# Operand buffers of layer 0's output projection: moved into layer 0's input space and kept open into layer 1

## The chip, the cores and the metric

The kernel runs on one core of one Trainium2 chip. The metric is the device time of one execution in microseconds; the comparison is between medians of several executions. The five engines are written as in the profile: PE (matmul), PEld (its weight load), DVE (vector), ACT (scalar), POOL (GpSimd), SP (sync, which here only issues loads).

## What is computed

Two layers of a diffusion trunk run over 128 context tokens and 1024 latent tokens, in float32. Around the change the work is this:

```python
# layer 0, output side; y_a from the SSD scan, y_b from the Hyena convolution
y_a = rms_norm(y_a * silu(z_a), norm_a_w)
xs  = xs + g_s * (concatenate([y_a, y_b], axis=-1) @ w_out)     # 2048 -> 1024
# layer 1, input side
h = rms_norm(xs, norm_w[1]) * (1.0 + sc) + sh
q, k, v, g = split(h @ w_in, 4, axis=-1)                        # 1024 -> 4 x 1024
# then 2-D neighbourhood attention with a bias table, o * silu(g), output projection,
# xs = xs + g_s * (...), final rms_norm
```

## The kernel before

**Numbers.** Every large product is made in three matmuls: an operand `x` is split into a high part (ACT's cast to `fp32r`) and a low part (DVE's subtraction `x - high`), and high·high, low·high and high·low are summed in PSUM. Weights stream in as 128x1024 blocks through two `wraw` buffers (`w_load`, L119); `w_split` (L125) makes their two halves (ACT L131, DVE L132). Activations are kept with channels on the partitions, as eight tiles of 128 x 1152 tokens.

**Buffers.** SBUF is handed out in pools, which are stacked from the left and from the right. A pool that is closed gives its bytes to the pools opened next; the first instructions that write into a new pool wait for all accesses to every pool whose bytes it takes, not only for those to the same bytes. Within a pool, a tag with `bufs=n` is a ring of n buffers, and a writer waits for the last use of the buffer that it gets.

**Order.** The program is emitted as one list. Before it goes to the chip, the queue of each engine is planned: in simulated time an engine takes, of what is ready, what was emitted first. On the chip each engine then works strictly through its queue. So a statement that is moved in the source changes who goes first where several things are ready. Loads are issued by SP, stores by POOL (`dma`, L85; `store`, L88).

**Start and layer 0.** `open` (L195) makes the pools that live throughout and loads the constants (`csq`, `pv`, `sel4`, `sel8`). Layer 0's input `h` is 16 tiles, `hh0`–`hh7` and `hl0`–`hl7`, in the pool `h` (53,120 to 126,848 bytes of each partition); products are evacuated through the pool `ev` above it (126,848 to 145,576). The last product of layer 0's input side is `x0g_main` (L894), which stores the eight tiles of the Hyena branch in `ybd`, apart from tile 6, which stays on the chip as `y6`. After its first group it calls `second` (L1587), and so `ssd_open` (L915), which loads the small mask `sm`, and starts the SSD scan (`ssd`, L976). The scan is a generator in the background list `bg`: `tick` (L92) advances it a few steps after each third of a product, so that DVE and ACT work on it while PE does the product.

**Output projection, stage out0a and out0b (L1602–1671).** `h` and `ev` are closed, and the pool `x1` takes the place: eight tiles of the residual stream, and the norm's small tiles and row scale `tt` with the diagonals `diag` (53,120 to 96,256). Behind it lie `yt` (two `yr` buffers, to 105,472) and `yb` (four `yhi` and four `ylo`, 105,472 to 142,336), so that `yb` reaches into the bytes of `ev`. `y_tile` (L1076) loads a tile of `y` into `yr` and splits it (L1086) into `yhi` and `ylo`. `out0` (L1096) runs over the four quarters of the 2048 input channels: quarter 3 and 2 from `ybd` (part 0 and 1), then the two of the scan (part 2 and 3), for which `mid` (L1612) drains the scan and builds its normalisation, and the pool `ya` on the right side holds eight split pairs. Each part runs over the eight output tiles `m`; `evac` adds the product times the gate to `x1[m]`. In part 2 the residual is loaded into `yr` and added (L1125).

**Layer 1's norm, in the last part.** `tail` squares each evacuated block of 384 columns into `sq1` (pool `yn`) and adds it up in `acc`. With the last output tile, per block: `token_sums` (L374) puts tokens on partitions, DVE makes the mean (`ms`), POOL the power -1/2 (`rs`), and `spread` (L362) brings it back to rows: DVE makes a diagonal (L366), PE multiplies it by ones (L369), ACT copies it out (L372). `tok(k)` (L1647, `to_tokens` at L698) turns an `x1` tile to tokens: nine PE transposes (L709), ACT's and DVE's copies (L712, L714) into `x1k` (pool `xk`), and a store to `x1d`, which the last stage of the kernel reads.

**Stage h1 (L1679).** Per tile `make_h` (L379) runs on DVE and ACT: two products with the row scale, into `sq` (L385, pool `hn`), ACT's high half, DVE's low half. The tiles `hh`, `hl` of layer 1 lie in the pool `h1` on the right. Behind the tiles 3 to 7 follows `tok(k)`.

**Stage qkv (L1208).** The pools of the output projection are closed, and `qk` and `at` are opened over them. `attn_open` (L1159) makes the two bias tables `Tb`: a memset of the whole table and one of its middle, for each half (L1165, L1166). For the first pair of heads `qkv` then makes the `q` and `k` weights, and splits the next two blocks, those of the value product, into the buffers of attention (`vw`, `QH`, `QL`), which aren't in use yet:

```python
if j == 0:
    first = [(evq, self.w_next(), [self.pj() for b in range(3)]),
             (evk, self.w_next(), [self.ps() for b in range(3)])]
    w = self.t(p_a, [128, 2, 1024], "vw", F32R, bufs=1)
    self.w_split(self.wpos, (w[:, 0], w[:, 1]))
    self.w_split(self.wpos + 1, [self.t(p_a, [128, 1024], n, F32R, bufs=1) for n in ("QH", "QL")])
    self.proj_k(first, self.hh, self.hl)
```

`proj_k` (L169) multiplies tile by tile as `make_h` delivers them (L186–188). Then `v_proj` (L1180) makes the values (L1191–1193) and attention runs in the background (`attn`, L1282; its context scores are L1330). `load_tables` (L1169) writes the windows of the bias into `Tb`.

Of the kernel before, what the change touches and what calls it, by code (L numbers as in the profile page):

```python
# [7 lines left out]
F32 = mybir.dt.float32  # L8
F32R = mybir.dt.float32r
AF = mybir.ActivationFunctionType  # L10
# [37 lines left out]
class Net:  # L48
# [146 lines left out]
    def open(self):  # L195
# [19 lines left out]
        self.dma(self.sel4, i["sel4"])  # L215
        self.sel8 = self.t(self.p_c, [128, 8], "sel8")
# [698 lines left out]
    def ssd_open(self, pool):  # L915
        nc = self.nc
        V = nc.vector
        sm = self.t(pool, [128, 12], "sm", bufs=1)
        self.dma(sm, self.i["sm"])
        self.sm = sm  # L920
        self.L = self.t(pool, [128, 8, 128], "L", F32R, bufs=1)
        self.Mv = self.t(pool, [128, 4, 128], "Mv", F32R, bufs=1)
        V.tensor_copy(self.L[0:64], bc(sm[0:64, 4:12].unsqueeze(2), [64, 8, 128]))
# [152 lines left out]
    def y_tile(self, src, k, p_y, pool, norm=None, r=None):  # L1076
        nc = self.nc
        if r is None:
            r = self.t(pool, [128, T], "yr")
            self.dma(r, src)  # L1080
        if norm is not None:
            nw = self.pv[:, PV["naw"] + k:PV["naw"] + k + 1]
            nc.vector.scalar_tensor_tensor(out=r, in0=r, scalar=nw, in1=norm, op0=ALU.mult, op1=ALU.mult)
        return self.split(r, p_y)

    def split(self, r, p_y, tags=("yhi", "ylo")):  # L1086
        nc = self.nc
        hi = self.t(p_y, [128, T], tags[0], F32R)
        lo = self.t(p_y, [128, T], tags[1], F32R)
# [118 lines left out]
    def qkv(self, p_a, p_q):  # L1208
# [3 lines left out]
        for j in range(8):  # L1212
# [11 lines left out]
            if j == 0:  # L1224
# [5 lines left out]
                self.w_split(self.wpos + 1, [self.t(p_a, [128, 1024], n, F32R, bufs=1) for n in ("QH", "QL")])  # L1230
                self.proj_k(first, self.hh, self.hl)
# [215 lines left out]
    def run(self, upto="end"):  # L1447
# [158 lines left out]
        x1 = [self.t(p_x1, [128, T], f"x1_{m}") for m in range(8)]  # L1606
        yst = ExitStack()
        pool = yst.enter_context(self.pool("yt", bufs=2))
# [3 lines left out]
        def mid():  # L1612
            self.drain()
            self.nd = 1
            rep = self.rstd_rep(self.ssq, p_x1, D)
# [12 lines left out]
        with self.pool("yb", bufs=4) as p_y:  # L1628
            self.label("out0a")
            ys = [self.y_tile(self.ybd[k], k, p_y, pool) for k in (4, 5, 7)]  # L1630
            ys.insert(2, self.y6)
            self.tick(self.EX)
            self.rate = self.RO
            self.out0(0, ys, x1, pool, order=(2, 0, 1, 3))
            ys = [self.y_tile(self.ybd[k], k, p_y, pool) for k in range(4)]
            self.out0(1, ys, x1, pool, mid=mid)
# [3 lines left out]
        acc = self.t(p_x1, [128, T], "tt", bufs=1)  # L1640
        psum = self.ps()
        ms = self.t(p_x1, [128, NCH], "ms", bufs=1)
        rs = self.t(p_x1, [128, NCH], "rs", bufs=1)
        self.nd = 1
        p_k = yst.enter_context(self.pool("xk", bufs=4))
        with self.pool("yn") as pn:
            def tok(k):  # L1647

                self.to_tokens(x1[k], self.x1d[:, :, k * 128:(k + 1) * 128].rearrange("c t n -> t c n"), p_k, "x1k", 4, both=True)()

            def tail(m, b, sl):
                if m == 0:
                    nc.scalar.activation(acc[:, sl], x1[m][:, sl], AF.Square)
                    return
                sq = self.t(pn, [128, NB], "sq1", bufs=3)
                nc.scalar.activation(sq, x1[m][:, sl], AF.Square)
                V.tensor_tensor(out=acc[:, sl], in0=acc[:, sl], in1=sq, op=ALU.add)
                if m == 7:

                    cs = slice(3 * b, 3 * b + 3)  # L1660
                    if b == 2:
                        tok(0)
                    self.token_sums(psum, acc, range(3 * b, 3 * b + 3))
                    V.tensor_scalar(out=ms[:, cs], in0=psum[:, cs], scalar1=1.0 / D, scalar2=EPS, op0=ALU.mult, op1=ALU.add)
                    nc.gpsimd.tensor_tensor(out=rs[:, cs], in0=ms[:, cs], in1=self.mh[:, cs], op=ALU.pow)
                    if b == 2:
                        tok(1)
                        tok(2)
                    self.spread(acc, rs, b, p_x1)

            self.out0(3, ya[4:], x1, pool, tail)
# [7 lines left out]
        with self.pool("hn") as pool:  # L1679
            self.label("h1")  # L1680
            self.hh, self.hl = [], []
            for k in range(8):
# [8 lines left out]
        with self.pool("at", bufs=2) as p_a:  # L1691
            self.attn_open(p_a)
# [218 lines left out]
```

## Time and profile before

| | us |
|---|---|
| runs | 2070.71, 2075.44, 2075.98 (median 2075.44) |
| profiled execution | 2070.57 |
| its span | 2068.8 |
| around the span | 1.77 |

| stretch (us from the start of the span) | work | PE busy |
|---|---|---|
| 840–1075 | `x0g`, the scan begins | 231.91 of 235.00 |
| 1075–1160 | out0a, the scan beside it | 82.28 of 85.00 |
| 1160–1327 | rest of the output projection | 161.19 of 167.00 |
| 1327–1358 | h1, first q and k products | 30.00 of 31.00 |
| 1358–1376 | the value product begins | 10.85 of 18.00 |
| 1376–1960 | values, attention, gates | 583.73 of 584.00 |

A row of a timeline gives the start, the mean duration, the engine, line and operation, output and inputs by the program's names, partitions times elements, how many such instructions are taken together, and in brackets how long the engine stood before it and what ended that. A row of the table by stretch gives, behind the length, the busy time and the count of instructions of PE, PEld, DVE, ACT and POOL, then the mean clock that was granted to PE (1.00 is full), the DMA engines' share and GB/s.

### The profile page before, as it was taken

The numbers are of one execution on the slowest core, as the hardware profiler recorded it, in microseconds if no ns is written. First come the engines' busy times: TensorE is split into PE (matmuls) and PEld (weight loads), VectorE is DVE, ScalarE is ACT, GpSimd is POOL, SyncE is SP. The second block draws the span as 40 slices with busy tenths as digits, with TensorE's granted clock in tenths as the row PEclk, the third lists the DMA queues.
The fourth block names the chain that finished last, engine by engine and source line by source line (L and its number), as shares of the span: only waits on it lengthen the run. The fifth ranks groups of instructions, "written<-read, shape, count | busy, mean of one in ns | idle before, by whom it ended". The sixth has DMA issues, their size and how long they took to land. (4 is left out here: it accounts for less than half of the span.)

```text
span 2068.8 us, 33792 instructions
## 1 busy us (share of the span) xinstructions
PE 2008.6 (97%) x13032; PEld 1815.4 (88%) x13032; DVE 1316.3 (64%) x2717; ACT 910.1 (44%) x2080; POOL 111.2 (5%) x235
## 2 busy tenths in 40 slices
PE   5999999999999999999999999989999999999998
PEld 3999997889999999888888899888888888888977
DVE  6887745146778787998899774743444444455374
ACT  4766642253333323554467411434544545454242
POOL 0010001110000000000000000100000000000000
PEclk9999999999999999999999999999999999999999
DMA  9142348554212113433343441233333233333362
GB/s 350 39 157 87 108 170 303 193 175 165 93 58 79 58 63 98 169 118 132 113 169 108 141 156 41 80 120 85 94 108 87 71 93 94 111 114 114 133 240 82
DMA packets 114344, 256.99 MB, mean 124 GB/s; under 512 B 27231, under 2 KB 62567, under 8 KB 111719
## 3 DMA queue, kind: packets, MB, share of 16 engines
q1 hardware_dynamic: 98872, 192.27, 28.9%
q0 software_dynamic: 15312, 62.57, 8.1%
q8 instruction: 103, 1.69, 0.3%
q14 instruction: 57, 0.47, 0.1%
HBM read 187.50 MB, written 67.28 MB: 123 GB/s over the span
## 5 line engine op out<-in xcount | busy, mean ns | idle before, releaser
L159 PE MATMUL pj<-hh,whi 128*128 128x384 f32 x1728 | 602.1, 348 | 3.4 <-DVE acc L880 2.9
L160 PE MATMUL pj<-hl,whi 128*128 128x384 f32 x1728 | 586.8, 340 | 0.0
L161 PE MATMUL pj<-hh,wlo 128*128 128x384 f32 x1728 | 586.4, 340 | 0.0
L159 PEld LDWEIGHTS pj<-hh,whi 128*128 128x128 f32 x1728 | 325.1, 188 | 25.0 <-issue 18.7
L160 PEld LDWEIGHTS pj<-hl,whi 128*128 128x128 f32 x1728 | 325.2, 188 | 7.5 <-issue 6.6
L161 PEld LDWEIGHTS pj<-hh,wlo 128*128 128x128 f32 x1728 | 324.7, 188 | 5.0 <-issue 4.2
L132 DVE TENSOR_TENSOR wlo<-wraw,whi 128x1024 fp32r<-128x1024 f32 x106 | 129.4, 1222 | 160.7 <-ACT whi L131 160.3
L131 ACT CAST whi<-wraw 128x1024 fp32r<-128x1024 f32 x106 | 111.1, 1049 | 247.8 <-PE pj L160 228.2
L1274 DVE CUSTOM_DVE_ANT_0 sz<-bg,Tb 128x512 f32<-128x512 f32 x128 | 83.5, 687 | 131.2 <-PE bg L1339 130.3
L613 ACT COPY raw<-pj 128x384 f32<-128x384 f32 (+2 forms) x140 | 55.9, 402 | 172.6 <-PE pj L161 83.8
L159 PE MATMUL pj<-yhi,whi 128*128 128x384 f32 x324 | 111.0, 343 | 1.4 <-DVE x L1110 1.4
L1276 ACT ACTIVATE sz<-sz,mx 128x512 f32<-128x512 f32 x128 | 91.6, 717 | 46.8 <-DVE mx L1274 46.4
L161 PE MATMUL pj<-yhi,wlo 128*128 128x384 f32 x324 | 110.4, 341 | 0.0
L160 PE MATMUL pj<-ylo,whi 128*128 128x384 f32 x324 | 109.2, 337 | 0.0
L1370 ACT COPY Pt<-bg 128x512 f32<-128x512 f32 (+1 forms) x144 | 71.8, 548 | 32.8 <-PE bg L1368 29.0
L1368 PE MATMUL bg<-csq,sz 128*128 128x128 f32 x528 | 73.9, 280 | 0.0
L942 ACT ACTIVATE xw<-xt,wd 128x64 f32<-128x64 f32 x256 | 64.5, 336 | 8.7 <-PE bg L949 8.0
L1368 PEld LDWEIGHTS bg<-csq,sz 128*128 128x128 f32 x528 | 56.7, 141 | 13.1 <-issue 13.0
L1110 DVE SCALAR_TENSOR_TENSOR x<-pj,mod,x 128x128 f32<-128x128 f32 (+1 forms) x96 | 46.6, 512 | 28.3 <-PE pj L161 24.3
L159 PEld LDWEIGHTS pj<-yhi,whi 128*128 128x128 f32 x324 | 60.9, 188 | 4.0 <-issue 3.3
L1191 PE MATMUL pj<-whi,hh 128*128 128x256 f32 x216 | 63.3, 293 | 0.0
L161 PEld LDWEIGHTS pj<-yhi,wlo 128*128 128x128 f32 x324 | 60.9, 188 | 1.3 <-issue 1.2
(445 smaller groups left out, 4073.2 us busy)
## 6 DMA issues: line engine op xcount, KB each, us to landing
wraw<-in_we SPq DMA_DIRECT2D x52, 512.0 KB, 3.4
wa<-in_wadg SPq DMA_DIRECT2D x32, 512.0 KB, 6.6
wraw<-in_wo SPq DMA_DIRECT2D x24, 512.0 KB, 3.5
Tb<-Cd SPq DMA_DIRECT2D x256, 48.0 KB, 2.0
Hd<-H POOLq DMA_DIRECT2D x8, 1280.0 KB, 5.2
H<-Hd SPq DMA_DIRECT2D x8, 1280.0 KB, 6.9
xt<-xtd SPq DMA_DIRECT2D x17, 512.0 KB, 4.2
wraw<-in_woe SPq DMA_DIRECT2D x16, 512.0 KB, 3.6
```

Of the source, the lines that this page charges most:

```text
L131: self.nc.scalar.copy(hi, r)
L132: self.nc.vector.tensor_tensor(out=lo, in0=r, in1=hi.bitcast(F32), op=ALU.subtract)
L159: nc.tensor.matmul(p[:, :NB], wh, xh[k][:, sl], start=(k == 0), stop=False)
L160: nc.tensor.matmul(p[:, :NB], wh, xl[k][:, sl], start=False, stop=False)
L161: nc.tensor.matmul(p[:, :NB], wl, xh[k][:, sl], start=False, stop=(k == nk - 1))
L613: nc.scalar.copy(raw[:, d], p[:, lo:hi])
L942: nc.scalar.activation(xw[:, h * 64:h * 64 + 64], x[:, h * 64:h * 64 + 64], AF.Copy, scale=self.wd[:, c, o:o + 1])
L1191: nc.tensor.matmul(p[:, :256], self.hh[k][:, ts], hi[:, q:q + 256], start=(k == 0), stop=False)
L1274: V.tensor_tensor_reduce(out=z[:, :n], in0=s, in1=tb, scale=-1.0, scalar=3.0e38, op0=ALU.add, op1=ALU.min, accum_out=m1)
L1276: nc.scalar.activation(z[:, :n], z[:, :n], AF.Exp, bias=m1, scale=-1.0, accum_out=sm)
L1368: nc.tensor.transpose(pt[:, b * 128:(b + 1) * 128], p[:, b * 128:(b + 1) * 128], self.ident)
L1370: nc.scalar.copy(t[:, :nb * 128], pt[:, :nb * 128])
```

## The change

Six edits go together.

1. `sm` is loaded in `open`, into the pool of constants, and no longer in `ssd_open`.
2. A pool `yb` is opened directly behind the eight `x1` tiles, so that it takes the second half of `h`'s bytes; the norm's small tiles go to a pool `xs` behind it. `yb` stays open until layer 1's input is made.
3. The first three `y` tiles (4, 5, 7) are loaded into `ylo` itself, and the low part is made in place. The others still go through `yr`.
4. The squares of `tail`, the row-scaled tiles of `make_h` and the token tiles take buffers of `yb` (`ylo`, `ylo`, `yhi`, four each) in place of pools of their own (`yn` with three, `hn` with two, `xk` with four).
5. A block's `spread` is emitted after the next block's sums; with the last block come blocks 1's spread, `tok(1)` to `tok(3)`, then block 2's spread. `tok(3)` no longer stands in h1.
6. `attn_open`, with its memsets, is emitted inside `qkv`, behind the two weight splits.

```diff
@@ open
+        self.sm = self.t(self.p_c, [128, 12], "sm")
+        self.dma(self.sm, i["sm"])
         self.sel8 = self.t(self.p_c, [128, 8], "sel8")
@@ ssd_open
-        sm = self.t(pool, [128, 12], "sm", bufs=1)
-        self.dma(sm, self.i["sm"])
-        self.sm = sm
+        sm = self.sm
@@ y_tile
+        if r is None and pool is None:
+            lo = self.t(p_y, [128, T], "ylo", F32R)
+            self.dma(lo.bitcast(F32), src)
+            return self.split(lo.bitcast(F32), p_y, lo=lo)
@@ split
-    def split(self, r, p_y, tags=("yhi", "ylo")):
+    def split(self, r, p_y, tags=("yhi", "ylo"), lo=None):
         hi = self.t(p_y, [128, T], tags[0], F32R)
-        lo = self.t(p_y, [128, T], tags[1], F32R)
+        if lo is None:
+            lo = self.t(p_y, [128, T], tags[1], F32R)
         nc.scalar.copy(hi, r)
         nc.vector.tensor_tensor(out=lo, in0=r, in1=hi.bitcast(F32), op=ALU.subtract)
@@ qkv
                 self.w_split(self.wpos + 1, [self.t(p_a, [128, 1024], n, F32R, bufs=1) for n in ("QH", "QL")])
+                self.attn_open(p_a)
                 self.proj_k(first, self.hh, self.hl)
@@ run, output projection
         yst = ExitStack()
+        p_b = yst.enter_context(self.pool("yb", bufs=4))
+        p_xs = yst.enter_context(self.pool("xs"))
         pool = yst.enter_context(self.pool("yt", bufs=2))
...
-            rep = self.rstd_rep(self.ssq, p_x1, D)
+            rep = self.rstd_rep(self.ssq, p_xs, D)
...
-        with self.pool("yb", bufs=4) as p_y:
-            ys = [self.y_tile(self.ybd[k], k, p_y, pool) for k in (4, 5, 7)]
+        ys = [self.y_tile(self.ybd[k], k, p_b, None) for k in (4, 5, 7)]
...
-            ys = [self.y_tile(self.ybd[k], k, p_y, pool) for k in range(4)]
+        ys = [self.y_tile(self.ybd[k], k, p_b, pool) for k in range(4)]
...
-                self.to_tokens(x1[k], ..., p_k, "x1k", 4, both=True)()
+            self.to_tokens(x1[k], ..., p_b, "yhi", 4, both=True)()
...
-                sq = self.t(pn, [128, NB], "sq1", bufs=3)
+            sq = self.t(p_b, [128, NB], "ylo", bufs=4)
...
                 nc.gpsimd.tensor_tensor(out=rs[:, cs], in0=ms[:, cs], in1=self.mh[:, cs], op=ALU.pow)
-                    if b == 2:
-                        tok(1)
-                        tok(2)
-                    self.spread(acc, rs, b, p_x1)
+                if b:
+                    self.spread(acc, rs, b - 1, p_xs)
+                if b == 2:
+                    for k in (1, 2, 3):
+                        tok(k)
+                    self.spread(acc, rs, 2, p_xs)
@@ run, h1
-        with self.pool("hn") as pool:
-                self.make_h(1, k, x1[k], acc, (pool, [128, T], "sq", F32, 2))
-                if k > 2:
-                    tok(k)
+            self.make_h(1, k, x1[k], acc, (p_b, [128, T], "ylo", F32, 4))
+            if k > 3:
+                tok(k)
@@ run, qkv
         with self.pool("at", bufs=2) as p_a:
-            self.attn_open(p_a)
             self.rate = self.RA
```

More of the change, by code (lines that the diff above doesn't have):

```diff
@@ L1626, in mid @@
                 ya_next()
-        with self.pool("yb", bufs=4) as p_y:
-            self.label("out0a")
-            ys = [self.y_tile(self.ybd[k], k, p_y, pool) for k in (4, 5, 7)]
[L1631 to L1634, printed above, removed]
-            ys = [self.y_tile(self.ybd[k], k, p_y, pool) for k in range(4)]
-            self.out0(1, ys, x1, pool, mid=mid)
+        self.label("out0a")
+        ys = [self.y_tile(self.ybd[k], k, p_b, None) for k in (4, 5, 7)]
+        ys.insert(2, self.y6)
+        self.tick(self.EX)
+        self.rate = self.RO
+        self.out0(0, ys, x1, pool, order=(2, 0, 1, 3))
+        ys = [self.y_tile(self.ybd[k], k, p_b, pool) for k in range(4)]
+        self.out0(1, ys, x1, pool, mid=mid)
         self.label("out0b")
@@ L1639, in run @@
         self.out0(2, ya[:4], x1, pool, each=self.ya_next)
-        acc = self.t(p_x1, [128, T], "tt", bufs=1)
+        acc = self.t(p_xs, [128, T], "tt", bufs=1)
         psum = self.ps()
-        ms = self.t(p_x1, [128, NCH], "ms", bufs=1)
-        rs = self.t(p_x1, [128, NCH], "rs", bufs=1)
+        ms = self.t(p_xs, [128, NCH], "ms", bufs=1)
+        rs = self.t(p_xs, [128, NCH], "rs", bufs=1)
         self.nd = 1
[L1645 to L1654, printed above, removed]
-                sq = self.t(pn, [128, NB], "sq1", bufs=3)
[L1656 to L1660, printed above, removed]
-                    if b == 2:
[L1662 to L1666, printed above, removed]
-                        tok(1)
-                        tok(2)
-                    self.spread(acc, rs, b, p_x1)
-            self.out0(3, ya[4:], x1, pool, tail)
@@ new lines, in tok, with tail @@
+        def tok(k):
+            self.to_tokens(x1[k], self.x1d[:, :, k * 128:(k + 1) * 128].rearrange("c t n -> t c n"), p_b, "yhi", 4, both=True)()
+        def tail(m, b, sl):
+            if m == 0:
+                nc.scalar.activation(acc[:, sl], x1[m][:, sl], AF.Square)
+                return
+            sq = self.t(p_b, [128, NB], "ylo", bufs=4)
+            nc.scalar.activation(sq, x1[m][:, sl], AF.Square)
+            V.tensor_tensor(out=acc[:, sl], in0=acc[:, sl], in1=sq, op=ALU.add)
+            if m == 7:
+                cs = slice(3 * b, 3 * b + 3)
+                if b == 2:
+                    tok(0)
+                self.token_sums(psum, acc, range(3 * b, 3 * b + 3))
+                V.tensor_scalar(out=ms[:, cs], in0=psum[:, cs], scalar1=1.0 / D, scalar2=EPS, op0=ALU.mult, op1=ALU.add)
+                nc.gpsimd.tensor_tensor(out=rs[:, cs], in0=ms[:, cs], in1=self.mh[:, cs], op=ALU.pow)
+                if b:
+                    self.spread(acc, rs, b - 1, p_xs)
+                if b == 2:
+                    for k in (1, 2, 3):
+                        tok(k)
+                    self.spread(acc, rs, 2, p_xs)
@@ L1672, in run @@
+        self.out0(3, ya[4:], x1, pool, tail)
         e2.close()
@@ L1678, in run @@
         self.p_h = hst.enter_context(self.pool("h1", right=True))
-        with self.pool("hn") as pool:
-            self.label("h1")
-            self.hh, self.hl = [], []
-            for k in range(8):
-                self.make_h(1, k, x1[k], acc, (pool, [128, T], "sq", F32, 2))
-                if k > 2:
-                    tok(k)
+        self.label("h1")
+        self.hh, self.hl = [], []
+        for k in range(8):
+            self.make_h(1, k, x1[k], acc, (p_b, [128, T], "ylo", F32, 4))
+            if k > 3:
+                tok(k)
         yst.close()
```

## The prediction

> **What bounds the kernel now.** I read the page's busy shares first, then busy time by stretch, then PE's timeline for its waits, then the other engines' timelines around the longest of them.
>
> ```profile
> span 2068.8 us, 33792 instructions
> PE 2008.6 (97%) x13032; PEld 1815.4 (88%) x13032; DVE 1316.3 (64%) x2717; ACT 910.1 (44%) x2080; POOL 111.2 (5%) x235
> ```
>
> PE is busy for 97% of the span, so the change can only shorten the time where PE waits or where its clock is low. After the stretches that the change touches, nothing gives a gain back: in the first stretch of attention PE is busy for all 40 us, and DVE for 17 of them.
>
> ```profile
> 1400.00:1440.00 40.00, 40.00 (x286) 34.91 (x286) 17.02 (x45) 19.49 (x45) 0.55 (x1) 1.00 0.35 97
> ```
>
> The longest wait of PE in the middle of the kernel is where layer 1's input product ends and the value product begins. PE's rows, then DVE's, ACT's, POOL's, and SP's waits between 1310 and 1375:
>
> ```profile
> 1358.95 0.34 PE L188 MATMUL bg<-hh,wlo 128*128 128x384 f32 x1
> 1359.55 0.59 PE L1191 MATMUL pj<-vw,hh 128*128 128x256 f32 x3 [0.27 <-issue]
> 1360.83 0.49 PE L1330 MATMUL bg<-kt,qt 64*128 64x128 f32 x4 [0.69 <-ACT kt L1222]
> 1367.52 0.58 PE L1192 MATMUL pj<-vw,hh 128*128 128x256 f32 x1 [6.20 <-DVE vw L132]
> ```
>
> ```profile
> 1353.22 0.68 DVE L712 COPY x1k<-bg 128x512 f32<-128x512 f32 x1
> 1358.94 2.62 DVE L1165 MEMSET Tb<- 128x3072 f32 x1 [5.05 <-PE bg L188]
> 1362.15 2.62 DVE L1165 MEMSET Tb<- 128x3072 f32 x1 [0.59 <-issue]
> 1364.88 1.50 DVE L1166 MEMSET Tb<- 128x768 f32 x2
> 1366.30 1.16 DVE L132 TENSOR_TENSOR vw<-wraw,vw 128x1024 fp32r<-128x1024 f32 x1
> ```
>
> ```profile
> 1358.41 1.05 ACT L131 CAST vw<-wraw 128x1024 fp32r<-128x1024 f32 x1 [0.15 <-ACT qt L1219]
> ```
>
> ```profile
> 1354.43 1.01 POOL L89 DMA_DIRECT2D x1d<-x1k  x1 [3.69 <-issue]
> ```
>
> ```profile
> SPq L86 <- DMA x1d<-x1k: 37.3, 4, 26.8
> ```
>
> PE stands for 6.20 us until DVE has made the low half of the first value weights, and DVE comes to that only after four memsets of the bias tables. DVE itself had stood for 5.05 us. The row blames PE, but the pool that holds the tables and these weights takes over the bytes of pools that still feed the last token store: DVE copies tile 7 until 1353.90, POOL issues its store at 1354.43, and ACT's cast and DVE's memset both start some 4 us after that, as SP's waits for the same store say. I call that moment, about 1358.4, the release.
>
> The stall also costs speed afterwards. The column behind the five engines is the granted clock:
>
> ```profile
> 1318.00:1320.00 2.00, 1.26 (x2) 0.73 (x3) 1.88 (x3) 1.02 (x2) 0.09 (x1) 0.67 0.04 8
> ...
> 1362.00:1364.00 2.00, 0.00 (x0) 0.00 (x0) 1.85 (x1) 1.09 (x2) 0.00 (x0) 0.76 0.41 107
> ...
> 1372.00:1374.00 2.00, 2.00 (x14) 2.00 (x14) 1.50 (x3) 1.06 (x3) 0.50 (x1) 0.68 0.40 86
> ```
>
> A mean of 0.76 over 2 us is 1.04 us at full and the rest at half, so the clock halved at 1363.04; 0.68 puts its return at 1373.28. PE worked from 1367.52 to 1373.28 at half speed, which is 2.88 us lost on top of the 6.20.
>
> **The change part by part.** It runs the same casts, subtractions, matmuls and transposes; it adds and removes no PE work. So the sum is one of waits.
>
> *The memsets behind the splits (attn_open inside qkv).* The framework plans each engine's queue ahead: an engine takes, of what is ready in the plan, what was emitted first (L1330 ran before L1192 above although attention is emitted later, being ready first). At the release DVE has nothing else, the first memset is ready, and the split is not, because ACT's cast of 1.05 us comes first. So I expect memset, both splits, then the other memset and the two short ones. The split then starts at 1358.94 + 2.62 = 1361.56 instead of 1366.30: a gain of 4.74 us. The bounds are 0 (all memsets still first) and 6.9 (split right behind the cast: 1358.41 + 1.05 + 1.16 = 1360.62 against 1367.52). I take 4.74, as the order follows from what is ready. The memsets that fall behind are waited for by the table loads on SP, which attention needs only after the value product, in the stretch quoted above; the next weights' loads on SP wait for the split's own buffer and come earlier. If that cover were gone, its price would be the 2.62 + 1.50 that moved.
>
> On the clock I count nothing. PE's remaining stall of about three microseconds, cut by the L1191 and L1330 matmuls, lies between 6.20, which halved the clock, and waits of 1.15 and 1.67 (below), of which the first stands with a halving; the bounds are a gain of 2.88 and a loss of about as much. The Trainium skill (TensorE: Matmul & The Clock Gate, Part 1) says that the gate looks at free-running windows of about 3.4 us, halves after an idle one and restores after a busy one. The trace agrees: 1363.04 to 1373.28 is 10.24 us, three such windows. By that rule a stall of one window still halves the clock in many of the executions, and the sum stays without this term.
>
> *The spreads one block later, tokens 1 to 3 ahead of the last.* PE and then DVE at the end of the output projection:
>
> ```profile
> 1318.74 1.65 PE L369 MATMUL bg<-diag,csq 128*128 128x384 f32 x2 [1.15 <-DVE diag L366]
> 1320.18 2.53 PE L709 MATMUL bg<-csq,x 128*128 128x128 f32 x13
> 1322.54 0.73 PE L377 MATMUL bg<-csq,tt 128*128 128x1 f32 x6
> 1323.13 1.73 PE L709 MATMUL bg<-csq,x 128*128 128x128 f32 x14
> 1326.53 0.88 PE L369 MATMUL bg<-diag,csq 128*128 128x384 f32 x2 [1.67 <-DVE diag L366]
> ```
>
> ```profile
> 1327.97 2.48 DVE L385 SCALAR_TENSOR_TENSOR sq<-x,mod,tt 128x1024 f32<-128x1024 f32 x2 [1.32 <-ACT tt L372]
> 1330.37 0.68 DVE L712 COPY x1k<-bg 128x512 f32<-128x512 f32 x1
> ```
>
> PE waits 1.15 and 1.67 us for the diagonals; 27 transposes (tiles 0 to 2) already run ahead of the last one, and the change lets nine more run in the second wait and tile 0's in the first. But PE's gain does not reach the value product by itself: the release hangs on DVE, which from 1327.97 to 1353.90 works through make_h and the token copies almost without a break. What counts is how much earlier DVE gets there. The copy of tile 3 (0.68 long, about 0.6 of queue) moves into the wait before make_h, and of the wait of 1.32 I give the half, 0.66: together 1.27 us. The bounds are -1.0 (nine transposes ahead of the last spread, 14 of which took 1.73 us, delay the rows' scale) and 3.1 (0.6 plus 2.5, were PE not at half clock at 1319 and both waits gone). I take the low middle, since the same diagonals still wait for the same pow.
>
> *First operand tiles split in place, pool inside the old input space.* PE, ACT, POOL, SP:
>
> ```profile
> 1075.71 0.77 PE L186 MATMUL pj<-yhi,whi 128*128 128x384 f32 x3 [1.16 <-ACT yhi L1090]
> 1083.10 0.80 PE L186 MATMUL pj<-yhi,whi 128*128 128x384 f32 x3 [0.56 <-ACT yhi L1090]
> ```
>
> ```profile
> 1074.46 2.21 ACT L1090 CAST yhi<-yr 128x1152 fp32r<-128x1152 f32 x2 [1.02 <-DMA ybd<-acc]
> ```
>
> ```profile
> 1069.43 0.54 POOL L89 DMA_DIRECT2D ybd<-acc  x1 [36.74 <-DVE acc L907]
> ```
>
> ```profile
> 1077.03 11.59 SPq L86 DMA_DIRECT2D yr<-ybd  x4
> ```
>
> Now the operand pool reaches into the evacuation pool, so the first casts wait for the last store out of that pool (issued 1069.43, landed by 1074.46) although their loads are in; and the third load waits for one of two yr buffers until 1077.03. With the operands inside the old input space and loaded straight into their low tiles, both waits go: 1.16 + 0.56 = 1.72 us at most. In this stretch DVE is nearly full, and what PE gains it can lose again when it drains the scan:
>
> ```profile
> 1080.00:1120.00 40.00, 39.23 (x218) 30.88 (x218) 36.61 (x84) 27.12 (x65) 0.90 (x1) 1.00 0.36 121
> ```
>
> So I count half, 0.86; the bounds are -1.3 (one subtraction of that length put ahead of the scan's) and 1.72.
>
> *sm loaded at the start.* DVE, PE, then SP at the start:
>
> ```profile
> 842.43 0.69 DVE L923 CAST L<-sm 64x1024 fp32r<-64x1024 f32 x1 [1.24 <-DMA sm<-in_sm]
> ```
>
> ```profile
> 846.09 0.44 PE L159 MATMUL pj<-hh,whi 128*128 128x384 f32 x1 [2.19 <-DVE acc L880]
> ```
>
> ```profile
> 1.66 0.90 SPq L86 DMA_DIRECT2D sel<-in_sel  x2
> ```
>
> DVE stands 1.24 us for this load, and behind it in DVE's queue are the operations for which PE then waits 2.19: 1.24 of these go. At the start one more issue of 0.90 / 2 = 0.45 us stands ahead of the first loads. Net 0.79, between -0.45 and 1.24.
>
> *Edits at nothing:* the norm's tiles in a pool of their own, x1k and the squares in operand slots, four buffers in place of two or three. The instructions are the same, and the slots' former users end some 100 us earlier.
>
> The sum is 4.74 + 1.27 + 0.86 + 0.79 = 7.66 us. The profiled execution took 2070.57 (1.77 around its span) and would take 2062.9. The runs were 2070.71, 2075.44 and 2075.98, and their median lies 4.87 above the profiled execution; for the median the same sum gives 2067.8.
>
> **The rivals.** *The order stays:* all memsets run before the split, if the plan finds the split unready twice. For it: they need nothing but the release. Against: ACT's cast of 1.05 fits into the first memset's 2.62. Then 2.92 remains: 2072.5.
>
> *The split goes first:* 6.9 in place of 4.74, and the stall, near 2 us, no longer halves the clock, another 2.88: 12.7 in all, 2062.7. For it: the emission order. Against: DVE stands idle and the memset is ready.
>
> *Slower:* moving sm makes the planner order the stretch from 840 anew, where DVE is the fullest engine beside PE. Its mechanism is the wait shown at 846.09: PE out of accumulators because DVE's gate product comes late behind scan work. Today it happens in one of eight groups. At 2.19 each it decides from the fourth new one on (8.8 against 7.66); in seven groups it costs 15.3, which gives 2083.1. Against it: emission order there is unchanged but for one load.
>
> *The change does not do what it says:* the first casts may still wait for the store, if the pool is not wholly inside the old input space. Eight x1 tiles and eight operand tiles take exactly the sixteen tiles of hh and hl, so I hold this for unlikely; it costs 0.86 of the sum, 2068.6.
>
> **How the numbers follow.** Forecast order 0.59, order unchanged 0.13, split first 0.17, does not do what it says 0.04, slower 0.07. About 0.3%, 6.2 us, is what a measurement of this kernel can tell from no change, so faster means below 2069.2. Of the forecast's 0.59 some 0.47 lies there, since clock, drain and the two levels of the runs (2070.7 and 2075.4) move it by several us; with 0.17 and 0.03 that is 0.67. Unchanged order and the rest of the forecast make 0.26, slower 0.07. The range goes from 2059, the split first in runs of the lower level, to 2075, where the order stays and the small gains fail.
>
> **What would show it.** Right: the wait before L1192 falls from 6.20 to 2 or less with one memset ahead of the split in DVE's timeline; no wait on the ybd store at L1090; no wait on sm at L923; the store of tile 7 is issued about a microsecond sooner relative to the last output product. Wrong: four memsets still ahead of the split, new waits of PE on L880 between 850 and 1075, or waits of PE in attention behind table loads.

## The result, and the profile after

The changed kernel takes 2057.36 us in the median of five runs (2055.94 to 2062.08) against 2072.03 for the kernel before (five runs, 2066.68 to 2075.98): the ratio is 0.9936, with a 95% interval of 0.9922 to 0.9950, so 10 to 16 us are gained. (The median before was 2075.44 over the three runs that the prediction had.) The prediction had 7.66 us and a range of 2059 to 2075. The sign was right; by the ratio the gain is about 13.3 us, 1.7 times the forecast, and the time lies below the range.

The profiled execution took 2058.23 us. From its page:

```profile
span 2056.5 us, 33778 instructions
PE 2002.8 (97%) x13032; PEld 1809.4 (88%) x13032; DVE 1316.9 (64%) x2717; ACT 909.8 (44%) x2080; POOL 111.5 (5%) x235
```

The work is the same, instruction for instruction on PE and DVE; PE's busy time is 5.8 us shorter for the same matmuls, which is speed, and the rest of the 12.3 us of span is waiting. To find the places, I compare when the same store is issued in both traces. POOL's timeline, before and after, for the first stored values and the last stored gate:

```profile
1384.90 0.76 POOL L89 DMA_DIRECT2D vd<-vt  x1 [10.86 <-ACT vt L1202]
...
1950.38 0.53 POOL L89 DMA_DIRECT2D gd<-vt  x1 [11.95 <-DVE vt L1251]
```

```profile
1375.63 0.76 POOL L89 DMA_DIRECT2D vd<-vt  x1 [10.15 <-ACT vt L1208]
...
1939.16 0.53 POOL L89 DMA_DIRECT2D gd<-vt  x1 [11.95 <-DVE vt L1258]
```

| moment | before | after | difference |
|---|---|---|---|
| scan's last store of `yad` | 1152.84 | 1153.88 | +1.04 |
| first diagonal of layer 1's norm | 1315.49 | 1315.36 | -0.13 |
| first stored values | 1384.90 | 1375.63 | -9.27 |
| last stored gate | 1950.38 | 1939.16 | -11.22 |
| end of the span | 2068.8 | 2056.5 | -12.3 |

Nine of the twelve microseconds are won between 1315 and 1385, where they were looked for. Two more come in attention, where PE had no wait at all and I expected nothing, and one in the last product. What is above the first row is not the change's: kernels whose code up to there is the same as before lay between -1.0 and +2.5 us at that store.

The place of the long wait, in the timelines of PE, DVE and POOL after:

```profile
1360.14 0.51 PE L1197 MATMUL pj<-vw,hh 128*128 128x256 f32 x3
1360.58 0.49 PE L1337 MATMUL bg<-kt,qt 64*128 64x128 f32 x4
1361.00 0.39 PE L1198 MATMUL pj<-vw,hh 128*128 128x256 f32 x1
```

```profile
1350.02 0.68 DVE L714 COPY yhi<-bg 128x512 f32<-128x512 f32 x1
1351.06 1.28 DVE L393 SCALAR_TENSOR_TENSOR hl<-ylo,mod,hh 128x1024 fp32r<-128x1024 f32 x1 [0.36 <-ACT hh L392]
1356.20 2.62 DVE L1171 MEMSET Tb<- 128x3072 f32 x1 [3.86 <-DMA x1d<-yhi]
1358.74 1.16 DVE L132 TENSOR_TENSOR vw<-wraw,vw 128x1024 fp32r<-128x1024 f32 x1
```

```profile
1351.23 1.01 POOL L89 DMA_DIRECT2D x1d<-yhi  x1 [1.29 <-ACT hh L392]
```

The wait of 6.20 us has not become shorter, it is gone. DVE's order is the forecast one (memset, split, split, memset). But it begins 2.74 us earlier (1356.20 against 1358.94), because tile 7's token copy now runs before the last low half (1350.02, then 1351.06), where before it was DVE's last operation (1353.22), and its store is issued 3.20 us earlier. The granted clock in the same stretches as before (the column behind POOL's), and where it halves now:

```profile
1332.00:1334.00 2.00, 1.46 (x5) 1.11 (x6) 2.00 (x4) 1.68 (x4) 0.00 (x0) 0.76 0.12 45
1334.00:1336.00 2.00, 2.00 (x11) 2.00 (x10) 2.00 (x3) 0.59 (x1) 0.00 (x0) 0.50 0.00 0
...
1362.00:1364.00 2.00, 2.00 (x19) 2.00 (x18) 1.57 (x1) 0.38 (x3) 0.00 (x0) 1.00 0.84 315
```

At 1362 PE has full speed. The halving of 1318 has moved to 1333.03 and lasts the same 3.41 us, in a stretch where PE still has waits:

```profile
1318.70 0.88 PE L371 MATMUL bg<-diag,csq 128*128 128x384 f32 x2 [0.25 <-DVE diag L368]
1325.21 0.88 PE L371 MATMUL bg<-diag,csq 128*128 128x384 f32 x2 [1.37 <-DVE diag L368]
1329.69 0.66 PE L711 MATMUL bg<-csq,x 128*128 128x128 f32 x4 [1.14 <-ACT yhi L716]
```

Three more, of 0.40, 0.53 and 0.47 us, lie in the window of 3.41 us that ends where the clock halves.

In out0a the casts no longer wait for the store (issued at 1070.63, behind the first cast), but PE has other waits in their place (ACT's row, then PE's):

```profile
1069.04 1.15 ACT L1096 CAST yhi<-ylo 128x1152 fp32r<-128x1152 f32 x1
```

```profile
1078.74 0.41 PE L186 MATMUL bg<-yhi,whi 128*128 128x384 f32 x1 [0.59 <-DVE cp L1003]
...
1083.41 0.44 PE L187 MATMUL pj<-ylo,whi 128*128 128x384 f32 x1 [0.23 <-DVE ylo L1097]
...
1088.44 0.97 PE L1037 MATMUL bg<-Mv,L 128*128 128x512 f32 x2 [1.14 <-ACT x L1114]
```

Attention, in the groups by line between 1400 and 1930: the value product's second matmul, before and after. Its mean is 2 ns shorter, and those of the two others of the group are 2 and 1 ns shorter (293 to 291, 280 to 279); the matmuls beside them are as long as before, within 1 ns.

```profile
L1192 PE MATMUL pj<-wlo,hh 128*128 128x256 f32 x216 | 60.7, 281 | 0.0
```

```profile
L1198 PE MATMUL pj<-wlo,hh 128*128 128x256 f32 x216 | 60.3, 279 | 0.0
```

### The profile page after: what moved, and what is told of

Same layout as the page of the kernel before. It is cut to its first block, busy times and chain, and to the rows that moved or that the text cites. A ratio compares the mean times of both kernels' runs of the same rounds, so it can differ in the third digit from the quotient of the medians.

```text
span 2056.5 us, 33778 instructions
## 1 busy us (share of the span) xinstructions
PE 2002.8 (97%) x13032; PEld 1809.4 (88%) x13032; DVE 1316.9 (64%) x2717; ACT 909.8 (44%) x2080; POOL 111.5 (5%) x235
## 4 chain that ended last, share of the span: by engine, by line
PE 79%; DVE 7%; issue 5%; DMA 5%; ACT 3%; SPq 1%; POOL 0%; POOLq 0%; ACTq 0%; DVEq 0%
PE pj L159 14%; PE pj L160 14%; PE pj L161 14%; PE bg L1363 3%; PE bg L1375 3%; PE bg L1346 3%; PE pj L1197 2%; PE pj L1198 2%; PE pj L1199 2%; PE bg L814 1%; PE bg L813 1%; PE bg L509 1%; PE bg L512 1%; PE bg L510 1%; PE bg L511 1%
## 5 line engine op out<-in xcount | busy, mean ns | idle before, releaser
L160 PEld LDWEIGHTS pj<-ylo,whi 128*128 128x128 f32 x324 | 60.9, 188 | 1.5 <-issue 1.1
```

The lines of the kernel that those rows point to most:

```text
L160: nc.tensor.matmul(p[:, :NB], wh, xl[k][:, sl], start=False, stop=False)
```

## The experiments

Two theories stood after this. **Mine:** two causes share one stall, the memsets' order (edit 6) and an earlier release; each alone leaves a rest, and only together do they remove the stall and with it the slow clock. (The clock turned out not to go with the stall: see edit 6 alone.) The release in turn is moved by make_h's four buffers, not by the new order of spreads. **The rivals:** one of the two does it alone; or the order of the spreads moves the release. The table is what they ended in; "standing" is the sum of PE's waits from the last q/k product to the second value matmul (before: 0.27 + 0.69 + 6.20 = 7.16). The times at which the split starts are each execution's own, and at the end of the output projection the executions lie up to 3.4 us from the kernel before; waits can be compared, these times only roughly.

| kernel | tile 7's copy | split starts | standing | clock halved there | ratio, 95% |
|---|---|---|---|---|---|
| before | last | 1366.30 | 7.16 | 10.24 | 1 |
| edit 6 alone | last | 1359.94 | 2.34 | 0 | 0.9965 (0.9953–0.9978) |
| edits 1 to 5 | ahead of it | 1359.94 | 3.71 | 6.83 | 0.9982 (0.9970–0.9993) |
| edit 5 alone | last | 1367.33 | 7.58 | 6.83 | 0.9992 (0.9983–1.0001) |
| edits 2 to 4 | ahead of it | 1362.48 | 3.53 | 3.41 | 0.9989 (0.9980–0.9999) |
| edit 6 and four buffers | ahead of it | 1360.64 | 0 | 0 | 0.9960 (0.9945–0.9975) |
| changed, two buffers | last | 1359.98 | 3.14 | 3.41 | 0.9952 (0.9937–0.9967) |
| changed | ahead of it | 1358.74 | 0 | 0 | 0.9936 (0.9922–0.9950) |

**Edit 6 alone.**

```diff
         with self.pool("at", bufs=2) as p_a:
-            self.attn_open(p_a)
@@ qkv
                 self.w_split(self.wpos + 1, ...)
+                self.attn_open(p_a)
```

> Only edit 6 (attn_open behind the two weight splits), all else as before. Theory (two causes that have to add up: the order of the memsets, and an earlier release because tile 7's token copy no longer stands behind the last low half on DVE): DVE's queue becomes memset, split, split, memset, so the split starts 4.7 us earlier than before, but the release stays at 1358.4; PE's wait for it falls from 6.20 to about 1.5. Gain 4.7 us if the clock still halves there, 7.6 if it doesn't; the ratio lies at 0.9965 to 0.998. Rival 1 (the order is all of it): the wait is gone and the whole gain of 12 us is there, ratio 0.994. Rival 2 (the earlier release is all of it): less than 2 us, ratio above 0.999.

Median 2062.75 against 2069.47. PE's and DVE's timelines:

```profile
1358.02 0.59 PE L1191 MATMUL pj<-vw,hh 128*128 128x256 f32 x3 [0.28 <-issue]
1359.29 0.49 PE L1331 MATMUL bg<-kt,qt 64*128 64x128 f32 x4 [0.68 <-ACT kt L1222]
1361.16 0.38 PE L1192 MATMUL pj<-vw,hh 128*128 128x256 f32 x1 [1.38 <-DVE vw L132]
```

```profile
1357.41 2.62 DVE L1165 MEMSET Tb<- 128x3072 f32 x1 [5.04 <-PE bg L188]
1359.94 1.16 DVE L132 TENSOR_TENSOR vw<-wraw,vw 128x1024 fp32r<-128x1024 f32 x1
```

The order is as forecast: one memset, then the split, 2.53 us behind the release. The standing falls by 4.82 us, and in this execution the clock stays at 1.00: 7.7 us worked out, 6.7 between the medians. Both rivals fall: the order alone is neither all nor nothing, but it is the larger part.

**Edits 1 to 5, without edit 6.**

```diff
@@ on the changed kernel
-                self.attn_open(p_a)          # qkv
+            self.attn_open(p_a)              # run, ahead of qkv
```

> Edits 1 to 5 without edit 6: the four memsets stand ahead of the split again. Theory: the release comes 2.75 us earlier as in the changed kernel, the split starts about 7.4 us behind it, PE waits about 3 us in place of 6.20, and the clock still halves for 10.24 us. Gain 3 us there plus 1 to 3 us elsewhere: ratio 0.997 to 0.998. Rival 1 (the order is all of it): the wait stays at 6.2 and the gain is at most 2 us, ratio above 0.999. Rival 2 (the release is all of it): ratio 0.994 to 0.995.

Median 2065.46 against 2069.47.

```profile
1361.16 0.58 PE L1198 MATMUL pj<-vw,hh 128*128 128x256 f32 x1 [3.71 <-DVE vw L132]
```

The release is early, four memsets stand ahead, a wait of 3.71 us is left, and the clock halves, for two windows rather than three. The rest is as the theory had it; the ratio lies just above the expected one.

**Edit 5 alone** (spread one block later, tokens 1 to 3 ahead of the last).

```diff
-                    if b == 2:
-                        tok(1)
-                        tok(2)
-                    self.spread(acc, rs, b, p_x1)
+                    if b:
+                        self.spread(acc, rs, b - 1, p_x1)
+                    if b == 2:
+                        for k in (1, 2, 3):
+                            tok(k)
+                        self.spread(acc, rs, 2, p_x1)
```

> Only edit 5 (spread one block later, tokens 1 to 3 ahead of the last spread, so tok(3) leaves h1). Theory (the release is moved by the four buffers for the row-scaled tiles, not by this edit): tile 7's copy is still DVE's last operation in h1, its store is issued within 1 us of 1354.4, PE's wait for the value weights stays between 5.3 and 7 us; time within 2 us of before, ratio 0.999 to 1.001. Rival (this edit is what I had priced in the prediction at 1.27 us and what moved the release): the store is issued 2.5 to 3.2 us earlier and the wait falls to 3 to 3.7 us; ratio 0.9985 or less.

Median 2067.89 against 2069.47; no difference that can be told. DVE's last operation in h1, and PE's wait:

```profile
1354.24 0.69 DVE L712 COPY x1k<-bg 128x512 f32<-128x512 f32 x1
```

```profile
1368.55 0.58 PE L1192 MATMUL pj<-vw,hh 128*128 128x256 f32 x1 [7.39 <-DVE vw L132]
```

Tile 7's copy is still last, and the wait is even longer than the 7 us that I had allowed. By the clock of this execution the store is no earlier (issued at 1355.46), but the last output product also ended 3.39 us later than before (1320.98 against 1317.59). Counted from there, DVE's first memset comes at 38.99 us, against 39.75 with edit 6 alone, where the tail is as before: so this edit may move the release by up to about a microsecond. PE's last q/k matmul comes earlier by as much (38.60 against 39.74), and the wait is no shorter. It is not this edit that puts the copy ahead of the last low half.

**Edits 2 to 4, the buffers alone.**

```diff
+        p_b = yst.enter_context(self.pool("yb", bufs=4))
+        p_xs = yst.enter_context(self.pool("xs"))
...
-                self.make_h(1, k, x1[k], acc, (pool, [128, T], "sq", F32, 2))
+            self.make_h(1, k, x1[k], acc, (p_b, [128, T], "ylo", F32, 4))
```

> Only edits 2 to 4 (operand pool in the old input space and kept open, first tiles split in place, squares, row-scaled tiles and tokens in its buffers, four each). Theory: with four buffers in place of two DVE runs ahead with the row-scaled products, the low halves and token copies shift by one, and tile 7's copy goes ahead of the last low half: its store is issued about 3 us earlier (1351 to 1352), PE's wait for the value weights falls to 3 to 3.7 us, the clock still halves; and PE's waits of 1.16 and 0.56 for the first operands go. Gain 3 to 5 us, ratio 0.9975 to 0.9985. Rival (edit 5 moves the release): the store is issued at 1354.4 as before and only the 0.9 us of out0a remain, ratio 0.9995.

Median 2066.28 against 2069.47.

```profile
1348.94 0.69 DVE L712 COPY yhi<-bg 128x512 f32<-128x512 f32 x1
1349.99 1.28 DVE L391 SCALAR_TENSOR_TENSOR hl<-ylo,mod,hh 128x1024 fp32r<-128x1024 f32 x1 [0.36 <-ACT hh L390]
```

The copy has gone ahead of the last low half, with the spreads in their old order. The wait is 3.53 us as expected; the ratio lies a little above the expected one.

**Edit 6 and one figure:** make_h's tiles get four buffers in place of two, in their old pool.

```diff
-                self.make_h(1, k, x1[k], acc, (pool, [128, T], "sq", F32, 2))
+                self.make_h(1, k, x1[k], acc, (pool, [128, T], "sq", F32, 4))
```

> Edit 6 and one figure: the row-scaled tiles of make_h get four buffers in place of two; all else as before (no pool is moved, no spread, no split in place). Theory (order and release have to add up, and these two small edits hold both): tile 7's copy goes ahead of the last low half, the release comes 2.5 to 3 us earlier, one memset stands ahead of the split, PE's wait for the value weights is under 0.5 us, the clock stays at 1.00. Gain at that place 7.2 us of standing and 2.9 us of clock, 10 in all, ratio 0.9945 to 0.9957. Rival (the other edits are needed as well): PE waits 1.4 us or more as with edit 6 alone, ratio 0.9965.

Median 2062.41 against 2071.01.

```profile
1361.97 0.34 PE L188 MATMUL bg<-hh,wlo 128*128 128x384 f32 x1
1362.14 0.28 PE L1191 MATMUL pj<-vw,hh 128*128 128x256 f32 x1
1362.26 0.28 PE L1192 MATMUL pj<-vw,hh 128*128 128x256 f32 x1
```

PE passes from the last q/k matmul to the values without a gap: these two small edits remove the stall. In this execution the clock was halved for 6.83 us further ahead, at 1320.06, so its total shows less than the place gained. The ratio lies just above the expected one and can't be told from that of edit 6 alone (0.9965): what the four buffers add in time, the medians don't show.

**The changed kernel with two buffers.**

```diff
-            self.make_h(1, k, x1[k], acc, (p_b, [128, T], "ylo", F32, 4))
+        with self.pool("hn") as ph: ...
+                self.make_h(1, k, x1[k], acc, (ph, [128, T], "sq", F32, 2))
```

> The changed kernel with one thing put back: make_h writes its row-scaled tiles into a pool of its own with two buffers, as before. Theory (the four buffers moved the release): tile 7's copy is again DVE's last operation in h1, its store is issued about 2.5 us later relative to the last output product, PE waits 1 to 2 us for the value weights, and the clock stays at 1.00, since two to two and a half microseconds of standing didn't halve it with edit 6 alone. It loses 1 to 2.5 us against the changed kernel: ratio 0.994 to 0.9955. Rival (that the clock stayed in the run with edit 6 alone was luck): the clock halves for 3.4 us or more, 3 to 5 us lost, ratio 0.9955 to 0.9965. Rival 2 (the spreads or the pools moved the release): nothing is lost, ratio as the changed kernel's.

Median 2059.79 against 2071.01.

```profile
1358.01 0.62 PE L1197 MATMUL pj<-vw,hh 128*128 128x256 f32 x3 [0.56 <-ACT vw L131]
1361.20 0.39 PE L1198 MATMUL pj<-vw,hh 128*128 128x256 f32 x1 [2.58 <-DVE vw L132]
```

```profile
1362.00:1364.00 2.00, 2.00 (x14) 2.00 (x13) 1.30 (x3) 0.00 (x0) 0.00 (x0) 0.63 0.82 281
```

The copy is last again, and the stall is back with 3.14 us. So it is the four buffers that put the copy ahead of the last low half. The ratio is the expected one, but its interval overlaps the changed kernel's. On the clock my expectation failed: it halves at 1362.51. I come back to that below.

**Padding of 64 and of 128 bytes.** The two microseconds of attention appeared only in the kernels that hold `sm` among the constants (from the first stored values to the last gate 565.48 us before, 563.53 after, 563.55 with edits 1 to 5, 563.78 with two buffers, and 565.2 to 566.9 in the four kernels above without it). The tile takes 64 bytes, so every pool of the left side lies 64 further; the weight halves then start at 29,440 in place of 29,376, at 0 in place of 64 modulo 128.

```diff
+        self.pad = self.t(self.p_c, [128, 12], "pad")     # the other kernel: 28
+        nc.vector.memset(self.pad, 0.0)
```

> As before, with an unused tile of 48 bytes in the pool of constants (it takes 64), so that all pools of the left side lie 64 bytes further on; one tiny memset at the start is added, no load is moved. It asks where the 1.9 us come from that the two kernels with sm among the constants gained slowly between 1385 and 1950, in attention, where PE has no wait. Theory (the place of the weight buffers: their start goes from 64 to 0 modulo 128 bytes): the value product's matmuls of 256 columns take 279 ns in place of 281, the stretch between the first stored values and the last stored gate gets shorter by 1.5 to 2.0 us, and nothing else changes; ratio 0.999. Rival (the order of the instructions, which the other edits shift): the matmuls stay at 281 ns, the stretch is the same within 0.3 us, ratio 1.000.

> As the kernel with 64 bytes of padding, but with 128, so that the weight buffers start at 64 modulo 128 bytes again. Theory (the place modulo 128 counts): the value product's matmuls take 281 and 280 ns as before, the stretch from 1385 to 1950 is as long as before within 0.3 us, PE's wait in the last product stays at 1.3 us or more, ratio 0.999 to 1.001. Rival (any shift does it, or the added memset does): 279 ns and a ratio as with 64 bytes, 0.997 to 0.9985.

With 64 bytes the ratio is 0.9978 (0.9969 to 0.9987), with 128 it is 1.0009 (0.9998 to 1.0020). The same group of matmuls, 64 bytes first:

```profile
L1194 PE MATMUL pj<-wlo,hh 128*128 128x256 f32 x216 | 60.3, 279 | 0.0
```

```profile
L1194 PE MATMUL pj<-wlo,hh 128*128 128x256 f32 x216 | 60.9, 282 | 0.0
```

The stretch of attention takes 563.87 us with 64 bytes and 565.80 with 128. So it is the place that counts (29,376 and 29,504 are slower than 29,440), not the size of the shift, nor the added memset, nor the order of instructions. The three places fit a rule modulo 128, and no run tells that from one modulo 256. The medians put the padding at 2.7 to 6.4 us; the 1.6 us of attention and about 0.7 in the last product (PE's wait there is 0.69 us with 64 bytes, 1.51 with 128, 1.35 before) are what the trace shows, and where the rest lies I haven't found.

**Edit 1 alone** (`sm` among the constants).

```diff
+        self.sm = self.t(self.p_c, [128, 12], "sm")
+        self.dma(self.sm, i["sm"])
```

> Only edit 1 (sm among the constants, loaded at the start). Theory of the prediction: DVE's wait of 1.24 us for the load goes, PE's wait of 2.19 us behind it falls to about 1, the start costs 0.45: net 0.8 us; with the 64 bytes that it moves the pools on, 1.5 to 2.0 more in attention, so 2 to 3 us in all, ratio 0.9985 to 0.999. Rival (slower, as feared in the prediction: the stretch from 840 is ordered anew and PE waits more for the gate product): PE's waits at L159 behind the gate product add up to over 5 us, ratio above 1.001.

Ratio 0.9985 (0.9975 to 0.9994): the expected size, but not by the expected way. DVE's wait for `sm` is gone and PE's wait of 2.19 us has become 0.78. Between the stores at 835 and at 873, the scan's first, 2.3 us are won (-0.62, then -2.91); by the scan's third store 1.56 are given back. Edit 6 alone, with the code of before up to there, won 1.0 at the same place, so what is left of this term is within what executions differ by. What stays to the end is the 64 bytes: 1.78 us in attention.

**Three small edits:** edit 6, four buffers, 64 bytes of padding, on the kernel before.

> Three small edits on the kernel before: attn_open behind the splits, four buffers for the row-scaled tiles in their old pool, and 64 bytes of padding. Neither the operand pool, nor the splits in place, nor the order of the spreads, nor sm is touched. Theory (these three carry the change's gain): no wait for the value weights, clock 1.00 there, 279 ns in the value product; ratio 0.9930 to 0.9945, as the changed kernel's 0.9936. Rival (the other edits bring 1 to 3 us of their own): ratio 0.9945 to 0.996.

Median 2057.61 against 2068.62, ratio 0.9945 (0.9928 to 0.9962), just on the line between the theory and the rival. PE's timeline:

```profile
1358.68 0.34 PE L188 MATMUL bg<-hh,wlo 128*128 128x384 f32 x1
1358.86 0.28 PE L1193 MATMUL pj<-vw,hh 128*128 128x256 f32 x1
1358.97 0.28 PE L1194 MATMUL pj<-vw,hh 128*128 128x256 f32 x1
```

No wait for the value weights, full clock, 279 ns. From the scan's last store to the last gate it gains 12.30 us, the changed kernel 12.26. So these three carry most of the change, 11.4 us of 13.3 by the ratios. Pools, splits in place and spreads add nothing that can be told apart, but up to about 2 us of theirs can't be ruled out: the changed kernel's execution lost 1.7 us to the halving at 1333.03, which this one was spared.

This kernel and edit 6 alone also show what the four buffers are worth, both executions being at full clock from the output projection into attention. Counted from the end of the last output product, the second value matmul starts at 43.50 us with edit 6 alone and at 42.24 here: 1.26 us are won, not the whole 2.34 of standing that went. In the new order the last low half runs behind the copy, and PE's last q/k matmul starts later (39.74, then 41.95).

**Splits not in place**, the pool where the change puts it (one execution, 2061.66 us).

```diff
-        ys = [self.y_tile(self.ybd[k], k, p_b, None) for k in (4, 5, 7)]
+        ys = [self.y_tile(self.ybd[k], k, p_b, pool) for k in (4, 5, 7)]
```

> The changed kernel with the first three operand tiles loaded through yr again, not split in place; the pool stays in the old input space. One look, for PE's waits at the first operands (1.16 and 0.56 before, gone in the changed kernel). Theory (the place of the pool removed them): neither comes back at more than 0.5 us, though the third load is issued later. Rival (the loads straight into the low tiles removed them): a wait of 0.5 us or more for the first or third cast is back.

```profile
1071.94 10.39 SPq L86 DMA_DIRECT2D yr<-ybd  x4
```

```profile
1075.12 1.09 PE L1031 MATMUL bg<-csq,yo 128*128 128x128 f32 x4 [3.07 <-DVE yo L1027]
1078.86 1.33 PE L186 MATMUL pj<-yhi,whi 128*128 128x384 f32 x3 [2.23 <-ACT yhi L1096]
```

The rival is right. With the operand pool in `h`'s place the `yr` buffers have come to lie over `ev`, and now the loads wait for the stores out of it: SP issues them at 1071.94, where the kernel before did at 1064.06. By this execution, loading straight into the low tiles is what the new layout needs. Its clock was halved there for 10.24 us from 1073.97, so its total says little more.

**One improvement on the changed kernel:** the token stores of tiles 0 to 3 issued by SP.

```diff
-            self.store(dst, o)
+            (self.dma if sp else self.store)(dst, o)      # sp = k < 4
```

> The changed kernel with one improvement: the token stores of tiles 0 to 3 are issued by SP and not by POOL, so that POOL's power for the last block doesn't stand behind the store of tile 0, which takes POOL 1.06 us to issue. Theory: the power starts about 1 us sooner, PE's wait for the last diagonal falls from 1.37 to 0.3 to 0.7, and the rest of h1 moves up by as much; 0.5 to 1.5 us in all, too little for the medians: ratio 0.9925 to 0.9945 (the changed kernel had 0.9936). Rival (the stores stand in SP's queue ahead of weight loads, which come late): PE waits for weights in h1, 1 us or more slower than the changed kernel, ratio above 0.9945.

```profile
1323.00 0.89 PE L371 MATMUL bg<-diag,csq 128*128 128x384 f32 x2 [0.25 <-DVE diag L368]
```

The wait for the last diagonal falls from 1.37 to 0.25, and in this execution the clock no longer halves at 1333. From the scan's last store to the last gate the gain is 13.71 us against 12.26; the halving that is gone accounts for 1.7, so the shorter wait itself doesn't show in that stretch. The median, 2056.59, with a ratio of 0.9940 (0.9924 to 0.9956), can't be told from the changed kernel's.

## Why the prediction was wrong

**The memsets' order: right.** The forecast order is there, and edit 6 alone puts the split 2.53 us behind the release and takes 4.82 us of standing away, against 4.74.

**The clock: wrong.** "On the clock I count nothing" is the first step that failed: 2.88 us belonged in the sum. It rested on a remaining stall of about three microseconds. My own terms for this place left less: 4.74 and 1.27 from one stall of 7.16 is 1.15. I added the terms and then judged the clock as if only the first were there. And even the 2.34 us that edit 6 alone leaves did not halve it, though that is one execution, in a window as busy as some that did halve (below), so it may be luck.

**"Edits at nothing": wrong.** Among them stood "four buffers in place of two or three". With four, DVE makes the scaled products of later tiles ahead, and its alternation of low halves and copies shifts by one, which brings the last copy ahead of the last low half. By the clocks of the two executions that moved the release by 2.74 us. Counted from the end of the last output product it came at 38.73 us against 41.35; but before, the clock had halved just there, and the kernels with the old order whose clock had not (edit 6 alone, edit 1 alone, the two paddings) have 39.75 to 40.65. So 1 to 2 us are the order's. The 1.27 us that I had given to the release I had from a different edit, the spreads. Alone they may have moved it by up to about that, but they shortened no wait for the value weights; in the changed kernel with two buffers the release came at 40.24, no earlier. And a token copy is not a matter of how much earlier DVE finishes: what releases the next stage is one particular store.

**The sum: wrong in form.** Order and release are not two amounts to be added; they draw on one stall. Together they exceed it (4.74 + 2.74 = 7.48 against 7.16), so it ends, and the clock's 2.88 come on top. 7.16 + 2.88 = 10.04 is what that place gave, less about 1 us that the new order costs ahead of it; the rival "the split goes first" had 2062.7 for this outcome, by another mechanism than the one that came.

**out0a: too high.** The casts' waits of 1.72 us are gone, waits of 0.59, 0.23 and 1.14 are new. From the scan's fifth to its last store the changed kernel gains 0.20 us, the buffers alone 0.57, where I had 0.86.

**sm: right place, wrong account.** The wait goes, and most of it is given back within the next 80 us. The rival that feared a new order there did not come. But the edit's 64 bytes gained 1.95 us in attention and shortened PE's wait in the last product, which is a term that nothing in the prediction had (after, then before):

```profile
1982.03 0.50 PE L1399 MATMUL pj<-whi,qt 128*128 128x512 f32 x1 [0.35 <-DVE ft L1424]
```

```profile
1994.33 0.50 PE L1392 MATMUL pj<-whi,qt 128*128 128x512 f32 x1 [1.35 <-DVE ft L1417]
```

**The account.** From the scan's last store on 13.3 us are gained: standing 7.16, clock 2.88, attention 1.95, the last product 1.1, the stretch from 1153 to 1315 1.17 (PE's waits there fell by about 0.6, the rest isn't settled), less about 1 us in the tail and h1, where the new order gives PE waits of 1.14, 0.40, 0.53 and 0.47 that it did not have in this form. Against the forecast the two terms that it lacked, the clock's 2.88 and about 3 of the 64 bytes, make about the difference of 5.6 us; the errors of the other terms nearly cancel, which is luck.

## What to carry to other kernels

Two gains that shorten the same stall are not a sum: work out what is left when both are there, and judge the clock by that rest. The number of buffers of a tile can decide in which order an engine's planned queue runs, even where no work changes, so look which single instruction releases the next stage, and what stands before it in the queue. When a stretch without any wait changes its length, compare the means of its instructions, and try the edit's shift of addresses by itself with a padding.

## What the runs showed of the hardware

**The clock's windows.** All halvings lie on one grid per execution, in steps of 3.413 us: in the kernel before, 1318.69 and 1363.06 are 13 steps apart. Before, the window that ended at 1363.06 held 0.98 us of matmuls (0.49 of the first values, 0.49 of L1330), 29% of it; with edits 1 to 5 it was 34%, in the changed kernel with two buffers 38% (2.10 us idle of 3.41). All three halved. With edit 6 alone the window, counted on from that execution's halving at 338.53, ran from 1359.12 to 1362.53 and held 1.55 us of idle time, 54% busy: no halving. But that is not a safe figure. In the same place a window that was 55% busy halved with 64 bytes of padding (1356.49 to 1359.90), and one of 54% with 128 (1355.57 to 1358.98). The Trainium skill (TensorE: Matmul & The Clock Gate, Part 1) has the halving after an idle window; here a window that is about half busy can be enough.

**Where the line lies.** Matmuls of few columns hardly count: before, the window that ended at 339.06 was wholly busy, 31% without the matmuls of fewer than 64 columns, and it halved. Without those, in the fourteen traces and between 300 and 2045 us, all 22 windows at full clock that were under 45.5% busy ended in a halving, and none of those of 57% or more did; of the 32 between, eight did. Near 845 us two windows of 45% differ: it halved with the three small edits (at 845.12), not before (844.24 to 847.65). What decides between 45% and 57% stays open.

**The same waits, another phase.** With edit 6 alone PE waits 0.17 and 1.14 us at 1315 and 1318, as before (0.17 and 1.15); before, the clock halved at 1318.69, there it did not. The windows lay 0.5 us differently and split the idle time: before, the one from 1315.27 to 1318.69 held 1.73 us of matmuls of 64 or more columns; with edit 6 alone, the two from 1314.74 to 1321.57 held 2.33 each. Such a halving costs 1.7 us, and executions of the same code can differ by it.

**The place of a moving operand.** A float32 matmul of 256 columns (the second of the value product's three) took 279 ns with its operand's buffers starting at 0 modulo 128 bytes and 281 to 282 at 64; matmuls that stream the other tiles were as long as before. 648 matmuls of the three kinds lie between 1400 and 1930, and by 2, 2 and 1 ns each they make 1.1 of the 1.95 us there. Why the place counts no run here shows.
